# More buffers for the units of h in the GDN features of a hybrid mixer layer, and fewer in the RWKV chain beside them

## The chip, the cores and the metric

The kernel runs on one core of a Trainium2 chip. The metric is the device time of one launch in microseconds (us). Before the change it is 4274.98 us, the median of 3 runs (4274.65 to 4275.81).

## The reference

One layer of a hybrid backbone works on 2048 latent tokens and 256 context tokens of width 1024. After adaLN modulation and an RMS norm, h is multiplied by one input projection, whose columns feed three mixers: gated DeltaNet (GDN), RG-LRU and RWKV-7. Their outputs go through an output projection, and a squared-ReLU MLP follows. All is float32. Cut to what matters here:

```python
qkv_l, z_l, beta_l, alpha_l, lx_l, lg_l, rw_l = split_last(hl @ p["w_in"], IN_SIZES)
# gdn_prep
qkv = jax.nn.silu(centred_conv(qkv, conv_w).astype(F32))
q, k, v = jnp.split(qkv, 3, axis=-1)
q, k, v = l2_normalize(heads(q)), l2_normalize(heads(k)), heads(v)
# rwkv_run, per token
S = S * w - einsum(S, kk) * (kk * a) + v * k
y = einsum(S, r)
```

GDN's features are q, k and v for all tokens. RWKV's recurrence is computed in 36 chunks of 64 tokens, both directions at once, with one state handed from chunk to chunk.

## The kernel before

After a front stage that makes h (kept in DRAM as `ht`) and RWKV's operands (`pk`, `vr` in DRAM), the function `mixed` (L1517) runs two instruction streams woven together on the same engines: RWKV's chain (`rwkv_mixer`, L1372) and GDN's features (`gdn_features`, L471). `weave` (L1504) advances the features by 1.15 pieces for every piece of the chain. The order of instructions on each engine and on SP's DMA queue is then fixed by a planner that simulates the program with its own costs: an instruction takes its place when its operands and its buffers are free in that simulation. On the chip every engine, and SP, keeps that order and waits where something is late.

**GDN's features.** `Proj.passes` (L372) runs 3 sets of columns (keys, queries, values) over 9 pieces of 256 tokens, 27 passes in all. A pass needs h of its piece: 8 slabs of 128 features, in 4 units of 2 slabs (`u=2`). For each unit `load` (L387) issues one DMA into a raw tile (L394), ScalarE (ACT) casts it to `hh` (L397), and GpSimd (POOL) subtracts to make the low part `hl` (L398). The raw tile and `hl` share one pool of slots, which is why both have the name hl in the profile:

```python
raw, hh, hl = self.raw(F32), self.hp.tile([128, self.u, PW], F32R, name="hh"), self.raw(F32R)
k.S.dma_start(out=raw, in_=k.d["ht"][:, q:q + self.u, o:o + PW])
```

With `hb=5` and `raw=5` there are 5 slots for hh and 5 for raw tiles and hl together. The 4 units of the running pass hold 4 of each until the last column tile of the pass has read them, and `load(p + 1)` is called as pass p begins (L383). The matmuls are `proj` (L419), three for each slab and column tile (hh by the high weights, hl by the high weights, hh by the low weights). The weights of the next set are staged through the same raw slots (L335, L359). In the third set the rows of v are written to DRAM (`kv<-rows`, L456) and then copied in reverse from DRAM to DRAM (`kv<-kv`, L464), both on SP's queue.

**RWKV's chain.** `chains` (L1189) calls `step(n)` for the 36 chunks. In step n, after its second part, it calls `load(n + 2)`. `load` (L1420) issues the DMA of `pk` (L1422), then, by `values` (L1411), three DMAs of V into the tile `sv` (L1415 to L1417), and goes on at once with the matmuls on pk (`rkp`, L1432, then `rbk`) and with `kw`, a product on GpSimd (L1446) that TensorE transposes into `kbn` (`rtp`, L1452). The tile sv holds V and the state of a chunk: step n reads it first in `z` (`rps<-sv,zl`, L1461), writes the next state into the tile of n + 1 (L1485), and reads its own for the last time in `rout` (L1492 and L1494). `gram` (L1399) loads `pb` (L1401) for the inverses, which run up to 12 chunks ahead. The pool `ld` (L1378) has 3 buffers for each of pk, pb, sv, zl, am and kbn; kw has 2.

Of the kernel before, what the change touches and what calls it, by code (L numbers as in the profile page):

```python
# [7 lines left out]
F32 = mybir.dt.float32  # L8
# [23 lines left out]
NCH = T // 64  # L32
# [228 lines left out]
def ada_rest(k, p, pp, tag):  # L261

    mc = p.tile([128, 2, KD], F32, name="mc")
    for i, j in enumerate((4, 3, 2)):
        for q in range(D // ADA_W):
            w = [p.tile([128, 4, ADA_W], F32, name=f"adw{a}") for a in range(2)]
            acc = ada_part(k, j, q, w)
            yield
            ps = pp.tile([128, 512], F32, name="adps", tag=tag)
            if i < 2:  # L270
                for m in range(ADA_W // 128):
                    for a in range(2):
                        k.mm(ps[:, m:m + 1], acc[a][:, 128 * m:128 * m + 128], k.ones[:, 0:1], a == 0, a == 1)
                m = slice(ADA_W // 128 * q, ADA_W // 128 * (q + 1))
                k.tt(k.V, mc[:, i, m], ps[:, 0:ADA_W // 128], k.pc["ada_b"][:, 8 * j + m.start:8 * j + m.stop], ADD)
            else:
                br = w[1][:, 1, :]
                ada_row(k, j, q, w, acc, ps, "norm_mix_post", br)
                k.S.dma_start(out=k.d["gp2"][:, ADA_W * q:ADA_W * q + ADA_W], in_=br)
        if i == 0:  # L280
            k.stt(mc[:, 0], mc[:, 0], 1.0, k.pc["norm_ffn_pre"], ADD, MUL)
        elif i == 1:
            k.S.dma_start(out=k.d["modc"], in_=mc)
# [187 lines left out]
def gdn_features(k, es, sm):  # L471

    d, tc, V, A, G = k.d, k.tc, k.V, k.A, k.G
    cw = k.pc["gdn_conv"]
    c4 = lambda v: v.rearrange("p r (n t) -> p r n t", t=64)
    pj = Proj(k, es, "g", u=2, hb=5, raw=5)
    w = es.enter_context(tc.tile_pool(name="gfw", bufs=2, side="right"))
    gt = chain(gates(k), decays(k, sm))
    rest = ada_rest(k, es.enter_context(k.tc.tile_pool(name="adr", bufs=1, side="right")), sm, "sm")

    def rows(p, y, a):
        to_rows(k, sm, w, d["kv"][0, :, 4 * p:4 * p + 4, a, :], y, "gsq")

    def normed(p, y, sq, s):

        scale = 64.0 if s else 1.0
        k.table("natural_log_exp_and_others")
        for a, b in ((0, 2), (2, 3)):
            ps = sm.tile([128, 2, 256], F32, name="gssq", tag="sm")
            for j in range(a, b):  # L490
                k.mm(ps[:, j - a, :], k.ones2, sq[:, j, :])
            k.act(sq[:, a:b, :], ps[:, 0:b - a, :], AF.Ln, scale=scale, bias=scale * 1e-6)
        k.act(sq, sq, AF.Exp, scale=-0.5)
        yk = w.tile([128, 4, 3, 64], F32, name="gyk", bufs=1)
        k.tt(V, yk.rearrange("p c j t -> p j c t"), c4(y), c4(sq), MUL)
        yr = w.tile([128, 4, 3, 64], F32, name="gyr", bufs=1)
        V.tensor_copy(yr, yk[:, :, :, ::-1])
        for dd, v in enumerate((yk, yr)):
            k.S.dma_start(out=d["kq"][dd, :, 4 * p:4 * p + 4, s], in_=v)
        yield  # L500
        if s == 0:
            k.tt(G, y, y, sq, MUL)
            rows(p, y, 0)
            yield

    before = None
    tiles = lambda c: [(c + 128 * j, 128) for j in range(3)]
    for s, p, h in pj.passes([tiles(GW) + [(C_BA, 24)], tiles(0), tiles(2 * GW)]):
        next(rest, None)
        y = w.tile([128, 3, 256], F32, name="gy")  # L510
        f0 = (3, 0, 6)[s]
        for j in range(3):
            ps = yield from pj.parts(j, h)
            k.act(y[:, j, :], ps[:, 0:256], AF.Copy, scale=cw[:, f0 + j:f0 + j + 1])
            for tap in range(1, 4):
                k.stt(y[:, j, :], ps[:, tap:tap + 256], cw[:, 9 * tap + f0 + j:9 * tap + f0 + j + 1], y[:, j, :], MUL, ADD)
            yield
        if s == 0:
            ps = yield from pj.parts(3, h, 2, 258)
            b = w.tile([24, 256], F32, name="gba", bufs=1)  # L520
            V.tensor_copy(b, ps[0:24, 0:256])
            k.S.dma_start(out=d["ba"][:, 256 * p:256 * p + 256], in_=b)
        if before:
            yield from normed(*before)
            before = None
        if s > 0:
            next(gt, None)
            next(gt, None)
        k.table("silu_and_others")
        k.act(y, y, AF.Silu)  # L530
        if s < 2:
            sq = w.tile([128, 3, 256], F32, name="gsq", bufs=1)
            k.tt(G, sq, y, y, MUL)
            before = p, y, sq, s
        else:
            rows(p, y, 1)
            backwards(k, lambda i: d["kv"][i, :, 4 * p:4 * p + 4].rearrange("p c a x -> p c (a x)"))
        yield
    yield from gt
# [832 lines left out]
def rwkv_mixer(k, es, ln, psg):  # L1372
# [5 lines left out]
    ld = es.enter_context(tc.tile_pool(name="rld", bufs=3))  # L1378
# [18 lines left out]
    units = [(u, par) for u in range(6) for par in range(2)]  # L1397

    def gram(n):  # L1399
        pb = ld.tile([128, 6, 2, 64], F32, name="pb")  # L1400
        k.S.dma_start(out=pb.rearrange("p u a t -> p u (a t)"),  # L1401
                      in_=d["pk"][:, n, :, :, 0:2, :].rearrange("p e r a t -> p (e r) (a t)"))
        ps = psg.tile([128, 6, 64], F32, name="rm", tag="sm")
        for u, par in units:
            h = half[par]
            k.mm(ps[h, u, :], pb[h, u, 1, :], pb[h, u, 0, :])
        for q, at, u, end in rounds.runs(6 * n, 6):
            A.copy(mu[:, at, :], ps[:, u, :])
            yield q if end else None

    def values(n):  # L1411

        sv = ld.tile([128, 4, 6, 64], F32, name="sv")
        to, vr = sv.rearrange("p a u x -> p a (u x)"), d["vr"][:, n].rearrange("p e x -> p (e x)")
        k.S.dma_start(out=to[half[1], 0:2], in_=vr[half[1]].unsqueeze(1).to_broadcast([64, 2, 384]))  # L1415
        k.S.dma_start(out=to[half[0], 2], in_=vr[half[0]])
        k.S.dma_start(out=to[half[1], 3], in_=vr[half[0]])  # L1417
        states[n] = sv

    def load(n):  # L1420
        pk = ld.tile([128, 6, 4, 64], F32, name="pk")
        k.S.dma_start(out=pk.rearrange("p u a t -> p (u a t)"), in_=d["pk"][:, n].rearrange("p e r a t -> p (e r a t)"))  # L1422
        values(n)
        if n == 0:
            for par in range(2):
                G.memset(states[0][half[par], 2 * par], 0.0)

        zl = ld.tile([128, 2, 6, 64], F32, name="zl")
        am = ld.tile([128, 2, 6, 64], F32, name="am")
        ps = psg.tile([128, 6, 64], F32, name="rkp", tag="sm")  # L1430
        for u, par in units:
            k.mm(ps[half[1 - par], u, :], pk[half[par], u, 2, :], pk[half[par], u, 0, :])  # L1432
        for par in range(2):
            h, o = half[par], half[1 - par]
            A.copy(zl[h, par], pk[h, :, 0, :])
            k.tt(V, zl[o, par], ps[o], mask(o, 0), MUL)

        ps = [psg.tile([128, 6, 64], F32, name=f"rbk{par}", tag="sm") for par in range(2)]
        for u, par in units:
            h = half[par]  # L1440
            k.mm(ps[par][:, u, :], pk[h, u, 1:3, :].rearrange("p a t -> p (a t)"), pk[h, u, 3, :])
        for par in range(2):
            k.tt(V, am[:, par], ps[par], mask(all_, 1), MUL)

        kw = ld.tile([128, 6, 128], F32, name="kw", bufs=2)
        k.tt(G, kw, pk[:, :, 1:3, :].rearrange("p u a t -> p u (a t)"),  # L1446
             k.wend[:, n].rearrange("p e r -> p (e r)").unsqueeze(2).to_broadcast([128, 6, 128]), MUL)
        kbn = ld.tile([128, 6, 128], F32, name="kbn")
        for dd in range(2):
            tp = psg.tile([128, 3, 128], F32, name="rtp", tag="sm")  # L1450
            for r in range(3):
                k.PE.transpose(tp[:, r, :], kw[:, 3 * dd + r, :], k.ident)  # L1452
            A.copy(kbn[:, 3 * dd:3 * dd + 3, :], tp)
        late[n] = am, zl, kbn, pk

    def step(n):
        am, zl, kbn, pk = late.pop(n)
        sv = states.pop(n)
        z = psc.tile([128, 6, 64], F32, name="rps")
# [39 lines left out]
        yield  # L1499

    return chains(k, rounds, gram, load, lambda q, m: ln.invert(mu, ys[q % 2], m, psl, True), step, 12, 2)


# [352 lines left out]
```

## Time and profile before

| | us |
|---|---|
| median of 3 runs | 4274.98 |
| the profiled execution's own time | 4250.58 |
| its span, first to last instruction | 4248.8 |
| TensorE matmul busy | 3616.1 (85% of the span) |
| VectorE busy | 2423.1 (57%) |
| GpSimd busy | 1685.2 (40%) |
| ScalarE busy | 1579.8 (37%) |

A time in a row is counted from the span's start. Engines are PE (TensorE matmul), PEld (its weight loads), DVE (VectorE), ACT (ScalarE), POOL (GpSimd) and SP, whose DMA queue is shown as SPq. A row of a list of waits says which instruction waited, after the arrow what released it, then the total in us, how often, and the longest. The chain of waits follows the work that ended last back from the end: each piece is what the next one waited for. The woven stage of chain and features lies between about 600 and 1770 us.

### The profile page before, as it was taken

Reading aid. Unit: us, or ns where it says so; the run is one execution under the profiler, and the core shown is the slowest. Engines: PE = TensorE matmul, PEld = TensorE weight load, DVE = VectorE, ACT = ScalarE, POOL = GpSimd, SP = SyncE. Lnnn points to the kernel's source line nnn. Section 1 sums busy time; section 2 is a strip of 40 time slices with the busy share of each in tenths; the row PEclk is TensorE's granted clock in tenths of the full one; section 3 lists DMA queues with packets and bytes.
Section 4 is the critical chain, followed back from the end, with each engine's and each line's share of the span. In section 5 each row is a group of like instructions: output and inputs, shape, how many; then the busy total and the mean of one; then the engine's idle time right before and its main releaser. Section 6 shows DMA issues by size and latency. Waiting matters only on the chain.

```text
span 4248.8 us, 75712 instructions
## 1 busy us (share of the span) xinstructions
PE 3616.1 (85%) x29914; PEld 3010.8 (71%) x29914; DVE 2423.1 (57%) x4389; ACT 1579.8 (37%) x3163; POOL 1685.2 (40%) x1589
## 2 busy tenths in 40 slices
PE   5888885888878776578696679989999999999998
PEld 3777775777767665577574457778888887888886
DVE  3576667747667362269969985643433337333334
ACT  3544443444454442233464535532222223221212
POOL 3343333344455443355585645422332224221212
PEclk8999896788778877798798669999999999999999
DMA  7433334344545544444364456631122124111112
GB/s 212 127 114 119 110 131 147 105 128 142 148 144 164 165 122 128 130 142 121 118 195 141 150 157 197 203 122 52 57 66 64 48 70 135 50 50 43 52 45 84
DMA packets 491797, 499.08 MB, mean 117 GB/s; under 512 B 38819, under 2 KB 443956, under 8 KB 491444
## 3 DMA queue, kind: packets, MB, share of 16 engines
q1 hardware_dynamic: 477620, 471.18, 36.4%
q0 software_dynamic: 5120, 16.78, 1.3%
q10 hardware_dynamic: 8704, 6.29, 0.5%
q8 instruction: 236, 3.87, 0.4%
q14 instruction: 117, 0.96, 0.1%
HBM read 368.45 MB, written 136.30 MB: 119 GB/s over the span
## 4 chain that ended last, share of the span: by engine, by line
PE 51%; DVE 21%; DMA 13%; ACT 5%; issue 5%; SPq 3%; POOL 2%; DVEq 0%; ACTq 0%; POOLq 0%
PE fdn L161 16%; PE fup L161 16%; PE proj L161 7%; PE opm L161 4%; DVE ltmp L135 3%; DVE yl L135 3%; DMA hl<-ht 3%; DMA pk<-pk 3%; PE rps L161 2%; DVE y L1138 2%; DMA ht<-mhh 2%; DVE pk L135 1%; PE gps L161 1%; DVE ml L1115 1%; PE rbk L161 1%
## 5 line engine op out<-in xcount | busy, mean ns | idle before, releaser
L161 PE MATMUL proj<-hh,whi 128*128 128x258 f32 (+2 forms) x2040 | 642.7, 319 | 120.2 <-ACT hh L397 62.7
L161 PE MATMUL proj<-hl,whi 128*128 128x258 f32 (+2 forms) x2040 | 630.2, 310 | 18.0 <-POOL hl L135 17.9
L161 PE MATMUL proj<-hh,wlo 128*128 128x258 f32 (+2 forms) x2040 | 624.6, 308 | 0.4 <-DVE wlo L135 0.4
L135 DVE TENSOR_TENSOR facc<-facc,fdn 128x512 f32<-128x512 f32 x480 | 326.3, 687 | 396.6 <-PE fdn L161 396.5
L161 PEld LDWEIGHTS proj<-hh,whi 128*128 128x128 f32 x2040 | 417.5, 207 | 154.6 <-issue 64.3
L161 PEld LDWEIGHTS proj<-hl,whi 128*128 128x128 f32 x2040 | 421.0, 207 | 36.3 <-POOL hl L135 19.3
L161 PEld LDWEIGHTS proj<-hh,wlo 128*128 128x128 f32 x2040 | 420.5, 206 | 16.7 <-issue 10.9
L135 POOL TENSOR_TENSOR hl<-hl,hh 128x520 fp32r<-128x520 f32 x216 | 296.9, 1381 | 335.1 <-ACT hh L397 250.7
L161 PE MATMUL fup<-fhh,uhi 128*128 128x512 f32 x1024 | 404.2, 395 | 5.6 <-ACT fhh L336 5.5
L161 PE MATMUL fup<-fhl,uhi 128*128 128x512 f32 x1024 | 403.2, 394 | 2.2 <-DVE fhl L135 2.2
L161 PE MATMUL fup<-fhh,ulo 128*128 128x512 f32 x1024 | 403.0, 394 | 0.0
L161 PE MATMUL fdn<-dhi,ah 128*128 128x512 f32 x1024 | 399.3, 391 | 4.0 <-ACT ah L1756 2.1
L161 PE MATMUL fdn<-dlo,ah 128*128 128x512 f32 x1024 | 399.2, 390 | 0.2 <-POOL dlo L135 0.2
L161 PE MATMUL fdn<-dhi,al 128*128 128x512 f32 x1024 | 395.0, 390 | 0.9 <-DVE al L135 0.9
L135 POOL TENSOR_TENSOR dlo<-draw,dhi 128x1024 fp32r<-128x1024 f32 x32 | 77.6, 2424 | 563.8 <-ACT dhi L336 543.6
L336 ACT CAST dhi<-draw 128x1024 fp32r<-128x1024 f32 x64 | 67.1, 1048 | 576.7 <-PE fdn L161 514.0
L135 POOL TENSOR_TENSOR fq<-fr 128x512 f32<-128x512 f32 x128 | 152.0, 1189 | 323.5 <-ACT fr L113 322.7
L397 ACT CAST hh<-hl 128x520 fp32r<-128x520 f32 x216 | 131.4, 624 | 299.6 <-DMA hl<-ht 279.5
L143 DVE SCALAR_TENSOR_TENSOR gy<-proj,parB,gy 128x256 f32<-128x256 f32 x243 | 113.5, 478 | 204.8 <-ACT gy L113 202.2
L161 PEld LDWEIGHTS fup<-fhh,uhi 128*128 128x128 f32 x1024 | 192.5, 188 | 50.9 <-ACT fhh L336 7.1
L161 PEld LDWEIGHTS fup<-fhl,uhi 128*128 128x128 f32 x1024 | 192.5, 188 | 47.7 <-DVE fhl L135 3.4
L161 PEld LDWEIGHTS fdn<-dhi,ah 128*128 128x128 f32 x1024 | 192.1, 188 | 48.0 <-ACT ah L1756 2.9
(368 smaller groups left out, 7907.8 us busy)
## 6 DMA issues: line engine op xcount, KB each, us to landing
hl<-ht SPq DMA_DIRECT2D x144, 260.0 KB
uraw<-in_ffn_up_dram SPq DMA_DIRECT2D x64, 512.0 KB
draw<-in_ffn_down_dram SPq DMA_DIRECT2D x64, 512.0 KB
pk<-pk SPq DMA_DIRECT2D x18, 1536.0 KB
pk<-pk SPq DMA_DIRECT2D x36, 768.0 KB
hl<-ht SPq DMA_DIRECT2D x36, 520.0 KB
pb<-pk SPq DMA_DIRECT2D x36, 384.0 KB
kqe<-kq SPq DMA_DIRECT2D x72, 192.0 KB
```

The source lines that it names most:

```text
L135: return e.tensor_tensor(out=out, in0=a, in1=b, op=op)
L143: return self.V.scalar_tensor_tensor(out=out, in0=a, scalar=s, in1=b, op0=op0, op1=op1)
L161: self.last = self.PE.matmul(out, l, r, start=start, stop=stop).ins
L336: k.A.copy(hi, raw)
L397: k.A.copy(hh[:, x, :], raw[:, x, :])
L1115: V.transpose(out=sw(ml[part]), in_=mu[part, :, cc].rearrange("p u i -> p i u"))
L1138: V.transpose(out=y[part, :, cc].rearrange("p u i -> p i u"), in_=sw(yl[part]))
```

## The change

GDN's features get 8 slots for hh and 8 for raw tiles and hl. In RWKV's chain pb and sv go from 3 buffers to 2 and kw from 2 to 1. V is no longer loaded in `load(n + 2)` during step n, but at the start of step n for chunk n + 1; only chunk 0 is loaded in `load(0)`. The computation and the number of instructions stay the same.

```diff
-    pj = Proj(k, es, "g", u=2, hb=5, raw=5)
+    pj = Proj(k, es, "g", u=2, hb=8, raw=8)
...
-        pb = ld.tile([128, 6, 2, 64], F32, name="pb")
+        pb = ld.tile([128, 6, 2, 64], F32, name="pb", bufs=2)
...
-        sv = ld.tile([128, 4, 6, 64], F32, name="sv")
+        sv = ld.tile([128, 4, 6, 64], F32, name="sv", bufs=2)
...
     def load(n):
         pk = ld.tile([128, 6, 4, 64], F32, name="pk")
         k.S.dma_start(out=pk.rearrange("p u a t -> p (u a t)"), in_=d["pk"][:, n].rearrange("p e r a t -> p (e r a t)"))
-        values(n)
         if n == 0:
+            values(0)
             for par in range(2):
                 G.memset(states[0][half[par], 2 * par], 0.0)
...
-        kw = ld.tile([128, 6, 128], F32, name="kw", bufs=2)
+        kw = ld.tile([128, 6, 128], F32, name="kw", bufs=1)
...
     def step(n):
+        if n + 1 < NCH:
+            values(n + 1)
         am, zl, kbn, pk = late.pop(n)
```

## Rows read from the trace of the kernel before

**Rows 1.** Busy time by stretch: us, then PE, PEld, DVE, ACT, POOL, clock, DMA share, GB/s.
```profile
1200.00:1500.00 300.00, 241.26 (x3051) 212.21 (x3051) 170.70 (x290) 148.94 (x285) 159.35 (x158) 0.80 0.53 157
1500.00:1770.00 270.00, 189.52 (x2501) 168.52 (x2502) 107.60 (x210) 86.16 (x175) 93.62 (x95) 0.79 0.41 120
```

**Rows 2.** Waits of PE, 680 to 1450 us, the first two sets.
```profile
PE proj L161 <- ACT hh L397: 9.4, 4, 5.1
```

**Rows 3.** Waits of PE, 1450 to 1770 us, the third set.
```profile
PE rkp L161 <- DMA pk<-pk: 27.8, 2, 14.6
PE proj L161 <- POOL hl L135: 17.0, 4, 13.8
PE proj L161 <- ACT hh L397: 14.0, 4, 11.4
```

**Rows 4.** The chain of waits by line, 680 to 1450 us.
```profile
by line: PE proj L161 14.0%; DVE ltmp L135 7.5%; DVE yl L135 7.4%; issue 5.8%; PE rps L161 5.1%; PE rbk L161 4.8%; DMA pk<-pk 4.8%; DMA hl<-ht 4.1%; DVE y L1138 4.0%; DVE gy L143 2.9%; DMA hl<-in_w_in_dram 2.6%; PE rtp L1452 2.5%; DVE ml L1
```

**Rows 5.** The chain of waits, 1450 to 1770 us: by line, and three pieces (start, us).
```profile
by line: DMA hl<-ht 14.6%; DMA pk<-pk 14.2%; PE proj L161 9.7%; issue 9.0%; DMA dm<-gb 5.7%; PE rps L161 3.8%; DMA kv<-rows 3.2%; DMA sv<-vr 3.0%; DVE ltmp L135 2.7%; PE rout L161 2.7%; DVE yl L135 2.4%; DMA adw<-in_ada_w_dram 2.3%; POOL hl
...
1467.21 18.24 DMA hl<-ht
...
1571.69 3.42 DMA hl<-ht
...
1673.32 19.16 DMA pk<-pk
```

**Rows 6.** Waits of SP's queue, 680 to 1450 us.
```profile
SPq L1422 <- PE rout L161: 61.3, 14, 15.8
SPq L394 <- PE proj L161: 59.4, 17, 16.6
SPq L394 <- POOL hl L135: 55.2, 22, 13.1
SPq L1401 <- PE rm L161: 40.8, 12, 11.5
```

**Rows 7.** Waits of ACT, 680 to 1450 us.
```profile
ACT hh L397 <- DMA hl<-ht: 91.8, 39, 5.8
...
ACT zl L1435 <- DMA pk<-pk: 26.9, 13, 3.4
```

**Rows 8.** Waits of ACT, 1450 to 1770 us.
```profile
ACT hh L397 <- DMA hl<-ht: 88.9, 19, 16.5
ACT zl L1435 <- DMA pk<-pk: 39.4, 6, 17.7
```

**Rows 9.** Groups by shape, 600 to 1800 us: busy us, mean ns, idle before.
```profile
L135 POOL TENSOR_TENSOR hl<-hl,hh 128x520 fp32r<-128x520 f32 x109 | 145.6, 1336 | 176.0 <-ACT hh L397 119.9 <-PE proj L161 23.5 <-ACT kbn L1453 10.9
...
L397 ACT CAST hh<-hl 128x520 fp32r<-128x520 f32 x112 | 69.7, 624 | 199.5 <-DMA hl<-ht 187.8 <-PE gdps L727 4.2 <-PE rbk L161 4.0
...
L161 PE MATMUL rps<-sv,zl 128*64 128x64 f32 x864 | 40.5, 233 | 0.1
```

**Rows 10.** SP's issues in order of time: start, us, line.
```profile
937.39 0.34 SPq L1422 DMA_DIRECT2D pk<-pk  x1
938.24 0.60 SPq L1415 DMA_DIRECT2D sv<-vr  x1
...
939.54 0.59 SPq L1417 DMA_DIRECT2D sv<-vr  x1
...
1631.10 0.65 SPq L464 DMA_DIRECT2D kv<-kv  x1
...
1672.57 0.66 SPq L464 DMA_DIRECT2D kv<-kv  x1
```

**Rows 11.** PE in order of time: `rout` of a chunk n−1, and `z` of chunk n+1.
```profile
1428.24 0.92 PE L161 MATMUL rout<-am,sv 128*64 128x64 f32 x24
...
1434.50 0.33 PE L161 MATMUL rps<-sv,zl 128*64 128x64 f32 x2
```

**Rows 12.** Waits of POOL, 680 to 1450 us.
```profile
POOL kw L135 <- PE rtp L1452: 28.2, 5, 13.7
```

## The prediction, made before the changed kernel was run

> **What bounds the kernel now.** I read first the busy time by stretch. The edits touch only the woven stage, about 600 to 1770 us, so I look at nothing else. In it no engine is full: TensorE is busy 241 of 300 us up to 1500 and 190 of 270 us after that, at a granted clock of about 0.8, with VectorE, ScalarE and GpSimd lower still [rows 1]. So the stage is held by waits that pass from engine to engine, and what counts is whose wait ends last.
>
> Next, TensorE's own waits for units of h. In the first two sets they are nearly nothing: 9.4 us on hh, of which 5.1 is one wait as the stage starts [rows 2]. In the third set they are 14.0 + 17.0 = 31.0 us [rows 3]. Together 40.4 us.
>
> Third, the chain of waits, because a late unit also harms indirectly. The DMA of h is 4.1% of 770 us, 31.6 us, in the first two sets [rows 4] and 14.6% of 320 us, 46.7 us, in the third [rows 5]: 78.3 us. The part that TensorE doesn't see itself comes through two in-order queues. SP stood at the h load for 59.4 + 55.2 us in the first two sets because no slot was free, with pk, pb and V queued behind it [rows 6]. ScalarE stood at the cast of h for 91.8 us and then 88.9 us, with the copies of the RWKV chain behind that [rows 7, 8].
>
> Why units are late: with 5 slots for raw tiles and hl together, the running pass holds 4, so the next pass gets one raw tile; its hl finds no slot until the last column tile of the running pass lets a unit go. Each unit then goes through load, cast (0.62 us) and subtraction (1.34 us) [rows 9] before its raw slot takes the next load. A load takes 3.4 us undisturbed, but 18.2 us where it stands behind the DRAM-to-DRAM copy kv<-kv [rows 5]. Undisturbed, a unit takes 3.4 + 0.6 + 1.3 = 5.3 us and four take 21 us.
>
> The page's cost says otherwise still more strongly. The Trainium skill, "DMA: Bandwidth & Descriptors", section "Anatomy of one DMA — SWDGE (gpsimd) path", gives about 2.0 us and the bytes at 436 GB/s, an estimate of 2.6 us for 260 KB; four units would then take 18 us of a pass of 41 us and five slots would do, so by that rule the sum below would lose its gain and end near 4283. The trace's 18.2 us contradicts it in the third set.
>
> **The change, part by part.**
>
> *Eight slots for hh and for raw tiles with hl.* Four are held by the running pass, four are free. The next pass can make hl of units 0, 1 and 2 and land the raw tile of unit 3 while the running pass still needs all its units; only the last subtraction (1.34 us) waits for a slot. A pass in the third set lasts 1672.57 − 1631.10 = 41.5 us [rows 10], more than 18.2 us behind a copy plus the rest. So TensorE's direct waits should go, except the 5.1 us at the start, where nothing can be ahead: at most 40.4 − 5.1 = 35.3 us. I don't count all of it. In the third set the copies kv<-kv, one a pass, stand in SP's queue, and each delays whatever is behind it: now h (18.2 us), now pk (19.2 us) [rows 5]. When h is no longer behind it at the wrong time, pk is next late; TensorE already waits 27.8 us for pk there [rows 3]. I take half of 31.0 = 15.5 us, and all of 9.4 − 5.1 = 4.3 us: about 20 us. Ends: 0 and 35.
>
> *The queues behind the h loads.* SP no longer stands at a load without a slot, and ScalarE reaches a cast whose load landed long ago. The chain shows 78.3 − 40.4 = 38 us of h that TensorE doesn't wait for itself. Much of that is replaced at once by another link (VectorE's inverse holds 7.5% + 7.4% of the chain in the first two sets [rows 4]), so I take a third: 12 us. Ends: 0 and 38.
>
> *V one step ahead instead of two.* The three issues move from behind pk(n+2) to the head of step n. Before, the slot of V(n+2) came free with rout of n−1 (three buffers); now the slot of V(n+1) comes free with rout of n−1 (two buffers). So V is issued at the same moment as now, but is wanted one step sooner, in z of n+1. Today z waits 0.1 us in all 36 steps [rows 9]. The shortest distance I find from a rout of n−1 to z of n+1 is 1434.50 − 1429.16 = 5.3 us [rows 11]; elsewhere it is most of a step, 1170 / 36 = 32 us on average. V's issues take 940.13 − 938.24 = 1.9 us [rows 10], and a landing like an h load's 3.4 us makes 5.3 us. So it fits, except behind a kv<-kv. Cost 0 here; the price elsewhere is in the rivals.
>
> *pk behind V.* Both wait for the same rout, and SP waits there for pk already 61.3 us [rows 6]. Now pk is issued at once [rows 10]; afterwards V's three issues come first, 1.9 us later for pk. Behind pk on TensorE stand rkp, rbk and rtp, and ScalarE's zl and GpSimd's kw wait for pk too. It costs at least 0 where pk is early, and at most 1.9 us in each of the 13 + 6 = 19 steps in which ScalarE waits for pk today [rows 7, 8]: 36 us. I take the steps in which TensorE itself waits: 2 in the third set [rows 3], and, counting the small ones before it, about 4, so 4 × 1.9 = 8 us.
>
> *pb and kw with a buffer less.* pb is loaded for chunks that run up to 12 ahead; SP waits for its slots 40.8 us already [rows 6] and will wait a little earlier in the row of grams. kw(n+1) must wait for the transposes of kw(n), a step before. GpSimd waits 28.2 us there today, half of it (13.7 us) at the start [rows 12]. Behind kw on GpSimd are the subtractions of h, which now have a pass of room: that is the cover. Cost 0; without it, from −2 (a different order at the start) to +5 us.
>
> **Sum:** −20 − 12 + 8 = −24 us. The profiled execution took 4250.58 us, 24.4 us (0.6%) less than the median; I take the difference over to the median: 4274.98 − 24 = 4251 us.
>
> **The rivals.**
>
> *All of it comes back.* Every piece of the chain that is an h load goes and no other link takes its place: −78 us, with the 8 paid −70, so 4205. For it: the two blocked queues. Against it: kv<-kv.
>
> *No change to measure.* In the third set the copies kv<-kv keep blocking the queue, whatever stands behind them, and the planner puts the casts of h early in ScalarE's order, so that ScalarE waits behind a copy for units that nobody needs yet. Left are 4.3 us in the first two sets and a few of the 12, against 8: 4275 − 4 = 4271, give or take 5. For it: an 18.2 us load right behind a copy is a load for the pass after next already [rows 5]. Against it: SP's 114.6 us of standing in the first two sets, where there is no copy. The Trainium skill, "DMA: Bandwidth & Descriptors", section "Queues, rings and completion order", says each DMA engine takes a ring's descriptors in order, SP having one ring on each; the 18.2 us agrees, and by that rule buffers alone don't get a load past a copy.
>
> *Slower: pk becomes the bound.* Place: SP's queue after each rout. V's issues come first and pk lands later; rkp follows in the same step and has no cover. It decides from the point where pk is late in all of the 19 steps: +36 us against −20 of direct waits is +16, 4291 us; where V also stands behind a copy and z waits, more.
>
> **How the numbers follow.** About 0.2%, 8.5 us, is what a measurement can tell from no change. Chances: the forecast 0.45 (own range 4230 to 4264), all back 0.12, no change 0.22, slower 0.21. With the forecast's edge giving a little to no change: faster 0.56, within 0.2% 0.22, slower 0.22. The range runs from 4202 (all back, nothing paid) to 4291 (the slower case).
>
> **What would show it.** Right: TensorE's waits for hh and hl in the woven stage near 5 us, SP's waits at L394 for slots a fraction of today's, DMA hl<-ht nearly gone from the chain. For the pk step: pk issued about 2 us after rout, with more waits of rkp. For V: z still with no wait. The forecast is wrong if h waits stay in the third set, or if they go and waits for pk, V or kw grow by as much.

## The result, and the profile after

The changed kernel takes 4214.03 us, the median of 4 runs (4210.2 to 4218.24), against 4275.4 us for the kernel before on the same chip: 0.9856 of it, with a 95% interval of 0.984 to 0.9872. That is 61 us less, where the forecast was 24. The time lies inside the stated range and on the side forecast, at over twice the forecast's size. On another chip the same two kernels gave 0.9854 (0.9839 to 0.9869).

Where it went shows in the stages of one profiled execution each. The woven stage is taken here from SP's issue of GDN's first weights (L335) to its issue of `colt`, the first load that needs the features whole (L1251); "rest" is from there to the MLP's first matmul.

| us | front | woven | rest | MLP | span |
|---|---|---|---|---|---|
| before | 669.5 | 1101.2 | 961.5 | 1516.6 | 4248.8 |
| changed | 676.8 | 1046.2 | 971.2 | 1514.4 | 4208.5 |
| changed, second run | 662.7 | 1046.6 | 971.3 | 1516.8 | 4197.4 |

The woven stage loses 55 us, and the rest, which nobody edited, gives 10 back. The front has the same code and differs by 14 us between the two profiles of the changed kernel, so that much of a span is no finding. The spans differ by 40 us and the medians by 61, since the profiled execution of before took 24.4 us less than its median.

Busy time of the woven stage by engine, columns as in [rows 1], first before:

```profile
669.55:1770.70 1101.15, 858.56 (x10954) 756.60 (x10956) 653.01 (x1193) 465.61 (x918) 479.28 (x486) 0.79 0.45 133
```

and the changed kernel:

```profile
676.76:1722.91 1046.15, 814.74 (x10954) 723.62 (x10956) 646.64 (x1193) 462.02 (x910) 477.64 (x481) 0.82 0.49 141
```

The matmuls are the same 10954. TensorE is busy 44 us less, at a mean granted clock of 0.82 instead of 0.79. The clock has two levels, 1.2 and 2.4 GHz, and of the stage 458 us were at the lower one before and 375 after (376 in the second run). A `proj` matmul takes 420 ns at the lower level and 283 at the upper (medians). TensorE's waits add up to 237.4 us instead of 251.5 (243.1 in the second run). So most of the 55 us is busy time of the same matmuls, not waits that went.

TensorE's waits in the changed kernel, the third set (1420 to 1725 us), beside [rows 3]:

```profile
PE rkp L161 <- DMA pk<-pk: 19.4, 2, 10.1
PE rps L161 <- DMA sv<-vr: 11.7, 1, 11.7
```

The waits for hh and hl have left the list. Over the whole woven stage two rows are left of them, against 40.7 us before:

```profile
PE proj L161 <- ACT hh L397: 1.1, 1, 1.1
PE proj L161 <- POOL hl L135: 0.9, 3, 0.4
```

New is one wait for V, 11.7 us. The queues, beside [rows 6 to 8]: SP in the first two sets (680 to 1420 us),

```profile
SPq L394 <- POOL hl L135: 94.7, 26, 13.9
SPq L394 <- PE proj L161: 55.9, 15, 17.5
SPq L1422 <- PE rout L161: 54.6, 13, 14.1
...
SPq L1401 <- PE rm L161: 32.8, 11, 8.8
```

and ScalarE in the third (1420 to 1725 us):

```profile
ACT hh L397 <- DMA hl<-ht: 70.7, 14, 13.6
ACT zl L1435 <- DMA pk<-pk: 58.5, 9, 14.9
```

In the first two sets SP stands at the loads of h longer than before, 94.7 + 55.9 = 150.6 us against 114.6. In the third it stands there 32.8 us, against 54.1 + 22.0 = 76.1 before, so over both 183 us against 191. In the third set ScalarE waits less for h and more for pk; in the first two it waits 99.5 us for h, against 91.8. GpSimd's wait for the transposes of kw, which has one buffer now, fell from 28.2 us [rows 12] to 15.0.

The chain of waits by line, 680 to 1420 us and 1420 to 1725 us, and three pieces of the second:

```profile
by line: PE proj L161 9.5%; DVE yl L135 7.6%; issue 7.3%; DVE ltmp L135 7.2%; DMA hl<-ht 5.8%; PE rps L161 3.9%; DMA pk<-pk 3.8%; DVE gy L143 3.5%; PE rbk L161 3.3%; DVE ml L1115 3.2%; DVE y L1138 2.5%; PE rout L161 2.3%; PE rtp L1452 2.2%;
...
by line: DMA pk<-pk 16.1%; DMA dm<-gb 14.0%; DMA hl<-ht 8.6%; PE proj L161 7.0%; issue 6.8%; DMA sv<-vr 5.7%; PE rps L161 5.5%; DMA hl<-in_w_in_dram 4.5%; PE rbk L161 4.4%; DMA kv<-rows 3.8%; PE rout L161 2.9%; PE rkp L161 2.3%; SPq L456 2.
...
1581.62 17.38 DMA sv<-vr
1629.26 16.03 DMA pk<-pk
1674.29 18.20 DMA pk<-pk
```

The loads of h hold 5.8% of 740 and 8.6% of 305 us, 43 + 26 = 69 us, against 78 [rows 4, 5]. In the third set pk, V and `dm` now stand where h stood.

### The profile page after: what moved, and what is told of

It reads as the page before. It is cut to its first block, busy times and chain, and to the rows that moved or that the text cites. A ratio compares the mean times of both kernels' runs of the same rounds, so it can differ in the third digit from the quotient of the medians.

```text
span 4208.5 us, 75743 instructions
## 1 busy us (share of the span) xinstructions
PE 3591.0 (85%) x29914; PEld 2997.3 (71%) x29914; DVE 2424.2 (58%) x4389; ACT 1574.5 (37%) x3163; POOL 1672.0 (40%) x1589
## 4 chain that ended last, share of the span: by engine, by line
PE 50%; DVE 22%; DMA 14%; issue 5%; ACT 5%; POOL 2%; SPq 2%; DVEq 0%; ACTq 0%; POOLq 0%
PE fup L161 16%; PE fdn L161 16%; PE proj L161 6%; PE opm L161 4%; DVE yl L135 3%; DVE ltmp L135 3%; DMA hl<-ht 3%; DMA pk<-pk 3%; PE rps L161 2%; DMA ht<-mhh 2%; DVE ml L1115 1%; DVE pk L135 1%; PE gps L161 1%; DMA dm<-gb 1%; DVE y L1138 1%
## 5 line engine op out<-in xcount | busy, mean ns | idle before, releaser
L135 DVE TENSOR_TENSOR al<-fq,ah 128x512 fp32r<-128x512 f32 x128 | 93.6, 732 | 229.9 <-ACT ah L1758 229.5
```

Source lines behind the costliest of these rows:

```text
L135: return e.tensor_tensor(out=out, in0=a, in1=b, op=op)
```

## The experiments

Each ratio is to the kernel before, on the same chip. "Woven" is the stage of the table above, from one profile each.

### Which part brings it

First the RWKV part alone, with 5 and 5 slots, and the same with the weights staged through three slots of their own, since the weights of the next set share the raw slots (L335).

```diff
e1_rwkv_only, from the changed kernel:
-    pj = Proj(k, es, "g", u=2, hb=8, raw=8)
+    pj = Proj(k, es, "g", u=2, hb=5, raw=5)
e2_weights_own3, from that: in weights(), instead of self.raw(F32)
+        return self.hp.tile([128, self.u, PW], F32, name="wst", bufs=3)
e3_weights_one, from the changed kernel: raw=7, and the same tile with bufs=1
```

> Only the RWKV part of the change; GDN keeps 5 slots of each kind. Theory W (the gain comes from the weights of the next set, which pass through the same raw slots at the two set changes) and rival H (it comes from the units of h within the passes): no gain, 4268 to 4290 us. Rival C (the later V loads and the new order of the chain gain by themselves): under 4250 us.

Measured: 0.9914 (0.9899 to 0.9928), −38 us, as rival C had it; woven 1066.3:

```profile
664.68:1730.99 1066.31, 848.36 (x10974) 742.88 (x10974) 662.64 (x1193) 464.69 (x920) 481.49 (x494) 0.82 0.46 138
```

The part that the prediction costed at +8 brings more than half of the gain, and the slots, from there on, 1066.3 − 1046.2 = 20 us of the stage, or 0.0059 × 4257 = 25 us by the ratios. The slots alone, on the chain as it was, were not run.

> 5 slots for hh and 5 for raw tiles with hl as before, but the weights of GDN's next set are staged through 3 slots of their own; the RWKV part as changed. Theory W: most of the 61 us is there, 4220 to 4245 us, and the weights of a set change are issued within about 10 us. Rival H: 4262 us or more.

Measured: 0.9877 (0.9858 to 0.9895); woven 1060.8. By the ratio that is in theory W's range, but W took e1 to bring nothing. Over e1, own slots for weights bring 5.5 us of the stage, and 16 us by the ratios.

> 8 slots for hh, 7 for raw tiles with hl, and one single slot of its own through which the weights of GDN's next set must pass one after another. Theory W: 20 to 45 us of the gain are lost, 4235 to 4260 us. Rival H: 4212 to 4225 us, as with all eight.

Measured: 0.9866 (0.985 to 0.9883); woven 1050.6, with 12.6 us of TensorE's waits for h, 11.5 of them put down to a load of h directly. With weights through one slot the changed kernel keeps nearly all. That the gain comes from the weights at the change of sets is out as the main cause.

### Which pool of slots

```diff
e4_raw8: hb=5, raw=8        e5_hh8: hb=8, raw=5        (else the changed kernel)
```

> All of the change, but hh keeps 5 slots; only raw tiles with hl get 8. The prediction's reason for late units is the pool that raw tiles and hl share: then this is as fast as the whole change, 0.983 to 0.988 of the kernel before. If the slots for hh matter as much: 0.989 to 0.993.

Measured: 0.9909 (0.9892 to 0.9926); woven 1068.1, waits for h 34.0 us. No gain over e1.

> All of the change, but raw tiles with hl keep 5 slots; only hh gets 8. By the shared pool this gains nothing over the RWKV part alone, which stood at 0.990 to 0.993 of the kernel before. If hh is what counts: 0.983 to 0.988.

Measured: 0.9832 (0.9815 to 0.985); woven 1049.0, waits for h 44.9 us. So neither pool alone takes TensorE's waits for h away, both together do; but this kernel, which has the waits, is no slower than the changed one. The stage's length doesn't follow these waits alone. By the ratios the pool that the prediction gave as its reason, raw tiles with hl, brings nothing over e1, and hh brings all of it; e8 and g1, below, say the opposite.

### What in the RWKV part

V moved alone, pb and kw cut alone, V moved with three buffers, V kept two steps ahead beside 8 raw slots, V issued behind pk, and the kernel before with V ahead of pk:

```diff
f1_v_only, from before: sv with bufs=2; values(n + 1) at the head of step(n)
f2_pb_kw, from before: pb with bufs=2, kw with bufs=1, nothing else
f1b_v_only_sv3: f1_v_only with three buffers of sv
e8_raw8_v2: f2_pb_kw with raw=8 (V two steps ahead, hb=5)
e6_v_behind_pk, from the changed kernel: V(n+1) issued in the middle of step n, behind pk(n+2)
p2_v_first, from before, in load(n):
+        values(n)
         k.S.dma_start(out=pk...)
-        values(n)
```

> Only V's loads move to the head of step n (sv with 2 buffers); pb, kw and GDN's slots as before. Theory V (the place of V's loads in SP's queue is what gains in the RWKV part): all of the 0.9% that the RWKV part alone gave, so 30 to 42 us less than the kernel before. Rival P (the smaller pools pb and kw, or any new order of the planner, do it): less than 15 us.

Measured: 0.9867 (0.985 to 0.9883), −57 us; woven 1063.7. More than theory V allowed, and 19 us more than all of the RWKV part (e1) brings.

> Only pb with 2 buffers and kw with 1; V two steps ahead and GDN's slots as before. Theory V: within 8 us of the kernel before, or slower. Rival P: 20 us or more less.

Measured: 0.9973 (0.9959 to 0.9987); woven 1079.0, the rest 987.1. That is −13 us, between the two expectations. Taking buffers away, and nothing else, makes the woven stage 22 us shorter, and the rest is 26 us longer than in the kernel before.

> 8 slots for raw tiles with hl (5 for hh), pb with 2 buffers, kw with 1, but V two steps ahead with 3 buffers as before. If slots and V's place add up, this gains what the whole change has over the RWKV part alone, 15 to 30 us. If the slots do all of it once they are there: 50 us or more. If the slots gain only together with V's new place: under 8 us.

Measured: 0.9862 (0.9848 to 0.9877); woven 1053.0, waits for h 17.8 us. At −57 us this meets the second expectation: with V where it was, the slots and the smaller pools bring as much as the whole change. Against f2 it is 26 us less in the stage and 44 us by the medians, for three more raw slots.

> All of the change, but V of chunk n+1 is issued in the middle of step n, behind pk of chunk n+2, instead of at the head of step n. If V ahead of pk costs what the prediction took (8 us): 4203 to 4209 us. If it costs nothing: 4210 to 4220 us. If V is then too late for z: over 4222 us.

Measured: 0.9834 (0.9818 to 0.985); woven 1047.4 against 1046.2. By the ratio this is where the first expectation lies, but the stage is the same, and what it is faster by comes in the rest (949.2 against 971.2), which this edit doesn't touch; over all these kernels the rest goes from 948.5 to 987.1 us. Nor does the pair test the price: in SP's order V(n + 1) stands ahead of pk(n + 2) in 2 of 34 steps of the changed kernel and in 1 of this one. The planner had put pk first in nearly every step already.

> Only V's loads move to the head of step n, for chunk n + 1, and sv keeps 3 buffers, so that V waits for no slot that the step before still holds. If V's later place gains by what stands behind it in SP's queue: as with 2 buffers, 0.985 to 0.989 of the kernel before, or a little faster. If it was the third buffer that did harm, by way of the planner's order: 0.995 or more.

Measured: 0.9955 (0.9939 to 0.9971), −18 us; woven 1085.6. The second expectation. With the third buffer the planner leaves V about where it was: the median V(n + 1) is issued 17.7 us ahead of pk(n + 2), against 16.3 in the kernel before, where in f1 it is issued 1.8 us behind it.

> The kernel before with V of chunk n + 2 issued ahead of pk of chunk n + 2 instead of behind it; nothing else. By the prediction's price of pk behind V: 8 us slower, at most 36 us slower. If the planner's order, which changes in thousands of places, counts for more: 10 us or more in either direction.

Measured: 0.9948 (0.9929 to 0.9967), −21 us; woven 1071.2. Faster, where the price said slower. But the edit hardly reached the queue: V stands ahead of its own pk in 4 of 36 chunks.

Put together: e1, f1, f2, f1b and p2 are five different small edits of RWKV's loads and buffers, all with 5 and 5 slots, and all shorten the woven stage, by 35, 37, 22, 16 and 30 us. They have no common part: f2 doesn't touch V, p2 and f1b take no buffer away. What they share is that the planner writes another order. Compared in the traces, 3173 (f1b) to 4344 (f1) of TensorE's 29914 matmuls and transposes stand elsewhere in the order than before; between the two profiles of the changed kernel 13 do. p2 and f1b are the clearest cases: what the edit asked for hardly happened, and the order moved all the same. The two in which V's loads did move, e1 and f1, are the two that gain most, 38 and 57 us against 13 to 21, so in this mode a part that comes from V's place is not ruled out.

### Is it the planner's order

If it is, the RWKV part should lose its worth where the planner orders in another way. The planner can also work without its simulation of time; `n_before`, `n_rwkv` and `n_after` are the kernel before, e1 and the changed kernel in that mode. `g1` joins the two quickest variants so far, e5 and e6: if their worth lay in the edits it should add up.

```diff
n_before, n_rwkv, n_after:
-    with tile.TileContext(nc, schedule_with_timeline_sim=True) as tc, ExitStack() as es:
+    with tile.TileContext(nc, schedule_with_timeline_sim=False) as tc, ExitStack() as es:
g1_hh8_v_behind: e6_v_behind_pk with hb=8, raw=5
```

> The kernel before, with the planner's other mode, which doesn't simulate times: another order of the same work. Expected slower than the kernel before, by 20 to 200 us; it is the base for the next two. Both theories say the same of it.

> The RWKV part alone (5 slots), in the planner's other mode. Theory N (the RWKV part has no gain of its own; the 28 us that every small edit of the chain brought came from a poor order that the kernel before happens to have): within 12 us of n_before, either way. Rival V (V's later loads gain by themselves): 25 us or more under n_before.

> The whole change in the planner's other mode. Theory N: the slots alone count, 15 to 40 us under n_rwkv. Rival V: less than 10 us under n_rwkv.

Measured: 1.018 (1.0151 to 1.021), 1.0264 (1.0244 to 1.0284) and 1.0246 (1.0226 to 1.0265) of the kernel before as it is: 4332.28, 4373.42 and 4361.54 us. In this mode the RWKV part costs 41 us, where it brought 38, and the whole change makes the kernel 29 us slower. Neither theory had that: N expected the part to be worth nothing, V a gain. The slots take 12 us away again by the medians, between what N and V expected. The woven stage lasts 1053.9, 1094.9 and 1061.6 us in the three, so by it the part adds 41 and the slots take 33; RWKV's last `rout` comes at 1817.3, 1859.3 and 1838.3 us, by which the slots take 21. TensorE's waits for h don't go here: 65.6, 94.7 and, with eight slots, 54.5 us.

> 8 slots for hh, 5 for raw tiles with hl, and V issued behind pk: the two fastest single variants together. If their gains are real and separate: 0.980 to 0.982 of the kernel before. If each was a lucky order: 0.983 to 0.988.

Measured: 0.9929 (0.9912 to 0.9946); woven 1085.6. Two edits that gave 0.9832 and 0.9834 give 0.9929 together, slower than both expectations.

### What holds the third set

```diff
e7_kv_act and e7_kv_pool, from the changed kernel, in the copy kv<-kv (L464):
-        k.S.dma_start(
+        k.A.dma_start(          (e7_kv_pool: k.G)
```

> The whole change, with the copy kv<-kv issued on ScalarE's queue. The same two theories: 0.976 to 0.982, or 0.983 and more; ScalarE then also stands until the rows of v have landed, 2 to 4 us in each of nine passes.

> The whole change, with the DRAM-to-DRAM copy kv<-kv issued on GpSimd's queue instead of SP's. If the copies' place ahead of pk, V and the other loads in SP's queue is what holds the third set once h no longer waits: the landings of 15 to 19 us right behind a copy vanish, and 15 to 40 us go from the whole change's 0.9855 (0.976 to 0.982). If the copies hold the DMA engines themselves, or GpSimd is held up by them: no gain, 0.983 or more.

Measured: 0.983 (0.9808 to 0.9853) on ScalarE's queue, the lowest time of all at 4176.77 us, and 0.9841 (0.9814 to 0.9868) on GpSimd's. Both intervals overlap the changed kernel's, so by the medians neither is told from it, and both lie where the second theory put them (0.983 and more). The traces say more on the waits. TensorE's matmuls on these loads in the woven stage, in groups by shape, in the changed kernel:

```profile
L161 PE MATMUL rkp<-pk 64*64 64x64 f32 x864 | 43.8, 248 | 32.7 <-DMA pk<-pk 24.6 <-DVE mc L135 4.6 <-ACT kbn L1453 3.4
L161 PE MATMUL rps<-sv,zl 128*64 128x64 f32 x864 | 42.3, 240 | 24.2 <-DVE zl L135 12.3 <-DMA sv<-vr 11.7 <-DVE sv L135 0.3
```

and with the copies on ScalarE's queue:

```profile
L161 PE MATMUL rkp<-pk 64*64 64x64 f32 x864 | 44.5, 250 | 11.6 <-DVE mc L135 4.7 <-ACT kbn L1453 3.7 <-DMA pk<-pk 3.2
L161 PE MATMUL rps<-sv,zl 128*64 128x64 f32 x864 | 44.3, 244 | 14.9 <-DVE zl L135 11.7 <-DVE sv L135 3.1
```

The waits for pk fall from 24.6 to 3.2 us and that for V goes. The third set, from the first copy to `colt`, in the changed kernel and then with ScalarE's queue:

```profile
1423.83:1722.91 299.08, 213.87 (x2734) 191.24 (x2736) 121.89 (x238) 97.55 (x201) 106.16 (x110) 0.77 0.42 125
```

```profile
1413.28:1681.37 268.09, 201.03 (x2728) 179.47 (x2728) 123.22 (x238) 97.62 (x201) 106.87 (x109) 0.82 0.47 140
```

31 us less, 13 of them TensorE's busy time at a higher mean clock; GpSimd's queue gives 287.2. The first two sets stay within 5 us of the second profile of the changed kernel, so the difference lies in the third set. That the copies' place in SP's order is its cause fits the waits but isn't shown: the planner's order changes here too (2216 matmuls stand elsewhere), on GpSimd's queue the waits for pk fall as well, to 6.2 us, and the stage only by 7 us, and by the ratios e7_kv_act is some 11 us faster, within the noise. The chain of that kernel, 1420 to 1680 us, shows what is late next: the copies themselves, and no landing of pk over 7.69 us.

```profile
by line: DMA kv<-kv 25.2%; PE proj L161 12.2%; DMA hl<-ht 11.0%; issue 6.7%; PE rps L161 6.5%; DMA pk<-pk 4.6%; PE rout L161 3.5%; PE rbk L161 2.5%; DVE ml L1115 2.3%; DMA kv<-rows 2.2%; PE nps L452 2.1%; PE rkp L161 1.8%; PE rtp L1452 1.7%
...
1613.18 7.69 DMA pk<-pk
```

## Why the prediction was right, and where it was wrong

**What failed: the terms for the RWKV chain.** "V one step ahead … Cost 0 here", "pk behind V … 4 × 1.9 = 8 us" and "pb and kw … Cost 0" sum to +8. Measured together (e1) they are −38 us by the medians and −35 in the stage. The step behind them that failed is to hold the rest of the order fixed: each term asked what three issues or one buffer do among instructions that stay where they are. The order isn't given by the source alone; the planner writes it anew from the buffers, and five unlike edits that leave the slots alone moved the stage by −16 to −37 us, while the same part cost +41 in the planner's other mode. So the 38 us are not the price of V's place or of pb and kw as the terms had it: p2 and f1b, whose edits hardly reached the queue, gain 21 and 18 us by order alone. How much of what e1 and f1 gain beyond that belongs to V's later place in this mode isn't shown. Every edit tried in the usual mode left a shorter stage than the kernel before, which speaks for a poor order there. Which of its waits makes it poor stays open: between before and e1 TensorE's waits fall by 251.5 − 225.0 = 26.5 us, in pieces (those of `rps<-sv,kbn` for the writes of sv from 24.4 to 7.3 us, while the waits for pk rise from 29.5 to 41.0).

**TensorE's waits for h: right.** Foreseen to go except the 5 us at the start; 40.7 became 2.0 us, 0.9 in the second profile, and the one at the start went too. The half taken off in the third set, for the copies, was not needed for these waits: they went there too, while pk (19.4 us) and V (11.7 us) are late behind the copies, as the step had it ("pk is next late"). The reason given, the pool that raw tiles share with hl, is half of it: with that pool alone at 8, 34.0 us stay (e4), and in the planner's other mode 54.5 us stay with both.

**The slots' worth: right in sign, its size not settled.** −20 − 12 = −32 was forecast. Like for like they give 20 us of the stage (changed against e1), 26 (e8 against f2, raw slots alone) and 33 (the other mode); by the medians or ratios 25, 44 and 12. All three pairs have the sign, but the reshuffling alone moves a stage by as much, e4 gains nothing over e1, and e5 reaches the changed kernel's stage with its 44.9 us of waits for h in place. Nor does it come as less waiting: against e1 (busy 848.4, waits 225.0) the changed kernel is busy 33.6 us less and waits 12.4 us more. What the slots do at each turn of the order is to make `proj` shorter. Its busy time in the stage (PE, PEld, DVE and ACT of `proj` alone) in e1, then in the changed kernel:

```profile
664.68:1730.99 1066.31, 378.32 (x2160) 315.13 (x2160) 115.01 (x249) 37.26 (x81) 0.82 0.46 138
676.76:1722.91 1046.15, 344.24 (x2160) 296.06 (x2160) 116.57 (x249) 37.26 (x81) 0.82 0.49 141
```

In the usual mode it is 373 to 382 us in all nine kernels with 5 raw slots and 344 to 357 in all seven with 7 or 8; in the other mode it falls from 384.5 to 373.0. Part of that is the clock: 485 of the 2160 start at its lower level in e1, 329 and 383 in the two profiles of the changed kernel. The prediction had no term for this. Why the slots have this effect, and why e4 has it (352.6) without a shorter stage, stays open.

**The queues behind the loads of h: the sign to look for was wrong.** SP's waits at L394 for slots were to be "a fraction of today's"; they rose from 114.6 to 150.6 us in the first two sets, fell from 76.1 to 32.8 in the third and are 183 us against 191 in all. h was to be "nearly gone from the chain" and holds 69 of 78 us. The step took the loads to stay where they stand in the queue while slots come free sooner; that the planner instead put them further ahead, so that SP waits there again, would explain it but isn't shown.

**pk behind V: it hardly happened.** The step says "afterwards V's three issues come first". In the changed kernel the planner put pk(n + 2) ahead of V(n + 1) in 32 of 34 steps, so there was nothing to pay for; TensorE's wait for pk fell from 29.5 to 24.6 us. What V ahead of pk costs where it does stand there no run measures alone: e6 and p2 change that order in a few steps only. The nearest is n_rwkv, with V ahead in 13 of 34 steps, where TensorE waits 1.7 us for pk. SP's issues of the changed kernel in order of time, pk(14) and V(13):

```profile
1073.94 0.34 SPq L1422 DMA_DIRECT2D pk<-pk  x1
...
1074.86 0.60 SPq L1415 DMA_DIRECT2D sv<-vr  x1
```

**V: right except behind a copy**, where the prediction placed its price: one wait of 11.7 us, and a landing of 17.38 us behind the copy issued at 1580.93. That z was to stay "with no wait" fails in a second way too: it waits 12.3 us for `zl`, which is not V. **kw and pb: no cost seen**, the waits on both got shorter.

**The rivals.** "All of it comes back" gave 4205, near the 4214 measured, by a mechanism that didn't happen: h stayed in the chain. Its time was met by another cause, which is luck. The range's lower end, 4202 for "all back, nothing paid", doesn't follow from its own terms: 4275 − 78 is 4197. "Slower: pk becomes the bound" fails on the waits for pk. "No change" fails on the time; the half of it that says the copies keep blocking the queue agrees with the waits in e7.

In e7 TensorE's waits for pk nearly went, and those for V went, once the copies had another queue. The Trainium skill, "DMA: Bandwidth & Descriptors", section "Queues, rings and completion order", has SP and ScalarE each own a row with one ring on each of the same 16 DMA engines, with descriptors taken in a ring's order; the fall from 24.6 to 3.2 us agrees. The rule of the Trainium skill that the prediction weighed, of 2.0 us and bytes at 436 GB/s ("DMA: Bandwidth & Descriptors", section "Anatomy of one DMA — SWDGE (gpsimd) path"), is stated there for DMAs issued by GpSimd, and these loads are SP's. By it five slots would do; the waits for h that went with the slots, 40.7 to 2.0 us, speak against it here.

Versions nominally ahead of the changed kernel are e7_kv_act (0.983), e5 (0.9832) and e6 (0.9834). Their intervals overlap its 0.984 to 0.9872.

## What to carry to other kernels

Where a planner writes the order, a change of buffers is a draw of a new order on every engine as well as the change that was meant: here it went with −16 to −37 us of the stage in five small edits, and the same part cost 41 us in the planner's other mode, as much as the eight slots brought or more. So allow for it in the range, and before crediting a mechanism run the parts alone, one edit that does nothing useful (f2 or p2 here), and the whole in another mode of the planner. Look, too, whether the order that was asked for is the one that the trace shows. A wait that disappears from the list is not yet time: look whether the stage gets shorter, what waits in its place, and whether it is the matmuls themselves that changed.

## What the runs showed of the hardware that was not expected

That a copy from DRAM to DRAM delays what stands behind it was in the prediction; that it delays much less what is on another queue was not. The copies move 768 KB each. On SP's queue pk landed 16.03 us after its issue, 4.8 us behind the issue of a copy, and 18.20 us after it, 1.9 us behind one, and V landed after 17.38 us. Elsewhere in the third set's chain of the same kernel, some 30 us behind a copy, pk landed after 4.2 to 6.1 us. With the copies on ScalarE's queue a pk issued 4.3 us behind a copy (1613.18) landed after 7.69 us, the longest in that chain, although the copies run beside it there too (19.79, 21.87 and 23.93 us in that chain). The bytes moved are the same; the DMA share of the stretch rises, from 0.42 to 0.47, as the stretch is shorter.
